# Sample tokens' low parts as extra columns of the first pass, in a split-float32 projection kernel

## The chip, the cores and the metric

The kernel runs on one core of a Trainium2 chip. The metric is the device time of one execution in microseconds. Times below are of the kernel before the change, from its timed runs and from one profiled execution.

## What is computed

One layer of a hybrid decoder on 256 prompt tokens and 8 single sample tokens (which come with a key/value window of 128 and with conv and SSM states), model width 2048, all in float32. Cut to what matters:

```python
def token_mixers(hn, pos, lw, state):
    proj = jnp.einsum('bld,de->ble', hn, lw['w_in'])
    q, k, v, z, xbc, dt_raw, gates = jnp.split(proj, SPLITS, axis=-1)
    q, k = rope(q, pos), rope(k, pos)              # 32 query heads, 8 key heads of 64
    attn = window_attn_...(q, k, v, sinks)         # window 128
    xbc_act, new_conv = causal_conv(xbc, conv_in, ...)
    y, h_last = ssd_chunked(...) or ssd_recurrent(...)
    y = gated_group_rms_norm(y + d_skip * xs, z, lw['ssm_norm'])
    attn_d = jnp.einsum('ble,ed->bld', attn, lw['w_attn_branch'])
    ssm_d = jnp.einsum('ble,ed->bld', y, lw['w_ssm_branch'])
    merged = sigmoid(g_attn) * attn_d + sigmoid(g_ssm) * ssm_d
    return jnp.einsum('bld,de->ble', merged, lw['w_out']), ...

def decoder_layer(x, pos, lw, state):
    mix, new_state = token_mixers(rms_norm(x, ...), pos, lw, state)
    h = x + rms_norm(mix, ...)
    g, u = split(rms_norm(h, ...) @ w_gate_up)
    return h + rms_norm((silu(g) * u) @ w_down, ...), new_state
```

## The kernel before

Activations lie with features on the partitions and tokens along the free axis: T = 264 columns, the NP = 256 prompt tokens first, then the NS = 8 sample tokens. A chunk is 128 features, so an activation of 2048 features is 16 tiles of 128x264.

All large products go through `gemm` (L143 to L187). A float32 product is made of three products of a shorter format: each weight piece is split into a rounded high part `hi` (a cast on ScalarE, L173, or L170 where heads are permuted) and the rest `lo` (a subtraction on VectorE, L174 or L171); each activation chunk likewise, when it is made, into a high tile (names in H: XH, HH, FH ...) and a low tile (XL, HL, FL ...), which `chunks` sets up and mostly `split` fills. For each output chunk m of 128 rows and each input chunk kc three matmuls accumulate in one PSUM tile: hi x high (L183), hi x low (L184) and lo x high (L185), 264 columns each. The low x low product is left out. A product (one call of `gemm`) has up to four output chunks, so it takes four PSUM tiles (name `g`); there are five such buffers. Weights come in pieces of 4 x 128 rows by 512 columns (`raw`, 3 buffers), and are split in halves of 128x1024 elements (4 buffers each for `hi` and `lo`).

In order of time: the pre-norm and the transposes of the input; the SSD branch's products (B, C, dt, x, z) with its conv and chunked scan, to 600 us; keys, values and queries from 600 us on, with the rotary embedding (`rope`), the prompt's attention and the sample tokens' recurrence beside them (both are generators of which `tick`, at each step of a product, lets some steps go ahead); the gates to 980 us; the SSM branch's projection (activations Y) to 1189 us; the attention branch's (A) to 1285 us; the output projection (M) to 1381 us, its norm; gate and up (H) from 1389 to 1915 us; the down projection (F) to 2177 us, the last norm and the output.

Readers of a finished `g` differ by stage: copies on ScalarE, the first conv step, and in the FFN a multiplication of gate and up on VectorE (L967 f). L309 and L477 are small copies of the 8 sample columns out of `g`.

The order of instructions on each engine is settled when the program is built, by the framework's scheduler, which simulates the engines and takes what it expects to be ready; an engine then runs its list in that order.

Of the kernel before, what the change touches and what calls it, by code (L numbers as in the profile page):

```python
# [5 lines left out]
F32R = mybir.dt.float32r  # L6
I32 = mybir.dt.int32
AF = mybir.ActivationFunctionType
ALU = mybir.AluOpType
# [23 lines left out]
def build(tc, I, O, wbufs=(3, 4, 4), gbufs=5, sbufs=((3,), (1, 2), (3,)), woff=0, aux="gpsimd", rr=1.4, pr=1.2, su=2, sr=1.0, hb=5, xbb=2, x0g=(0, 1, 2, 3), x0st="sync"):  # L33
# [81 lines left out]
    def chunks(pl, nm, n):  # L115
        r = [], []
        for c in range(n):
            for a, x in zip(r, "HL"):
                a.append(til(pl, [P, T], f"{nm}{x}{c}", 1, F32R))
        return r  # L120

# [21 lines left out]
    def gemm(W, segs, nk, X, perm_heads=False, perm_rows=False):  # L143
        XH, XL = X
        w = sum(n for _, n in segs)
        nch = w // P
        ps = [gps() for _ in range(nch)]
        for g0 in range(0, nk, 4):
            raw = til(wp, [P, 4, 512], "raw", wbufs[0])
            with tc.high_priority(offset=woff):  # L150
                o = 0
                for c0, n in segs:
                    src = W[g0 * P:(g0 + 4) * P, c0:c0 + n]
                    if perm_rows:
                        for j in range(2):
                            dma(raw[64 * j:64 * j + 64, :, o:o + n],
                                src[256 * j:256 * j + 256].rearrange("(i d) n -> d i n", d=64))
                    else:
                        last[0] = dma(raw[:, :, o:o + n], src.rearrange("(k p) n -> p k n", p=P))
                    o += n  # L160
                hl = []
                for b in range(2):
                    hi = til(wp, [P, 2, 512], "hi", wbufs[1], F32R)
                    lo = til(wp, [P, 2, 512], "lo", wbufs[2], F32R)
                    r = raw[:, 2 * b:2 * b + 2, :w]
                    if perm_heads:
                        for k in range(2):
                            rk = r[:, k].rearrange("p (j i d) -> p j i d", j=2, i=4)
                            hk, lk = (a[:, k].rearrange("p (i j d) -> p j i d", j=2, i=4) for a in (hi, lo))
                            S.copy(hk, rk)  # L170
                            V.tensor_tensor(lk, rk, fr(hk), ALU.subtract)  # L171
                    else:
                        S.copy(hi[:, :, :w], r)  # L173
                        V.tensor_tensor(lo[:, :, :w], r, fr(hi[:, :, :w]), ALU.subtract)  # L174
                    hl.append((hi, lo))
            for b in range(2):
                hi, lo = hl[b]
                for m in range(nch):
                    for k in range(2):
                        kc = g0 + 2 * b + k  # L180
                        wh, wl = (a[:, k, m * P:(m + 1) * P] for a in (hi, lo))
                        f, l = kc == 0, kc == nk - 1
                        PE.matmul(ps[m][:, :T], wh, XH[kc], start=f, stop=False)  # L183
                        PE.matmul(ps[m][:, :T], wh, XL[kc], start=False, stop=False)  # L184
                        PE.matmul(ps[m][:, :T], wl, XH[kc], start=False, stop=l)  # L185
            tick()
        return ps  # L187

# [1 line left out]
    win = I["w_in"]  # L190
# [11 lines left out]
    XHp = pool("xhat", side="right")  # L202
    XH, XL = chunks(XHp, "X", 16)
    SR = pool("srec")
# [47 lines left out]

# [1 line left out]
    ss = til(cp, [P, 3], "ss")  # L254
# [40 lines left out]
    A0.release()  # L295
    X = (XH, XL)

# [1 line left out]
    MS = til(cp, [P, 2, 8], "MS")  # L299
# [17 lines left out]
    def decays():  # L317
# [1 line left out]
        dtT = til(cp, [P, T], "dtT")  # L319
# [175 lines left out]

# [1 line left out]
    ps = sps()  # L497
# [13 lines left out]

# [1 line left out]
    cwb = lambda k: cw[:, k, :].unsqueeze(1).broadcast_to([P, NS, 48])  # L513
# [8 lines left out]

# [1 line left out]
    psum_phase(1)  # L524
# [65 lines left out]

# [1 line left out]
    def rope(pss, dsts):  # L592
# [47 lines left out]

# [1 line left out]
    QB = til(A4, [P, NS, 4, 8], "QB")  # L642
# [65 lines left out]

# [1 line left out]
    def sample_attention():  # L710
# [65 lines left out]

# [1 line left out]
    for dst, c0 in ((ts_d, C_GS), (ta_d, C_GA)):  # L778
# [9 lines left out]

# [1 line left out]
    psum_phase(2)  # L790
    YP = pool("yp", side="right")
    YH, YL = chunks(YP, "Y", 32)
    DP = pool("dproj", side="right")
# [12 lines left out]
    for u4 in range(4):  # L806
        for i, ps in enumerate(gemm(I["w_ssm_branch"], [(512 * u4, 512)], 32, (YH, YL))):
            m = 4 * u4 + i
            t = til(DP, [P, T], "ts", 3)
            ld(t, ts_d[m])  # L810
            V.scalar_tensor_tensor(t, t, 1.0, ps[:, :T], ALU.add, ALU.mult)
            st(m1_d[m], t)
        if u4 == 2:
            drain()
            SA.release()
            A4.release()
            AO = pool("attn_o")
            AH, AL = chunks(AO, "A", 16)
            for c in range(16):
                split(AF_[c], AH[c], AL[c])  # L820
    DP.release()
    YP.release()

# [1 line left out]
    MP = pool("merged", side="right")  # L825
    MH, ML = chunks(MP, "M", 16)
    DP = pool("dproj2")
    for u4 in range(4):
        for i, ps in enumerate(gemm(I["w_attn_branch"], [(512 * u4, 512)], 16, (AH, AL), perm_rows=True)):
            m = 4 * u4 + i  # L830
# [11 lines left out]

# [1 line left out]
    HP = pool("hp")  # L844
    HH, HL = chunks(HP, "H", 16)
    rb2 = til(HP, [P, T], "rb2")
# [28 lines left out]
    for u4 in range(4):  # L875
        for i, ps in enumerate(gemm(I["w_out"], [(512 * u4, 512)], 16, (MH, ML))):
            m = 4 * u4 + i
# [28 lines left out]

# [1 line left out]
    def gate(u4):  # L908
        sgs = []
        for ps in gemm(I["w_gate_up"], [(512 * u4, 512)], 16, (HH, HL)):  # L910
            sg = til(FT, [P, T], "sg", 8)
# [37 lines left out]
    FP = pool("fp", side="right")  # L949
    FH, FL = chunks(FP, "F", 44)  # L950

# [8 lines left out]
    for u4 in range(11):  # L960
        if u4 > 1:
            sgs.append(gate(u4))
            if u4 < 10:
                keep(u4 - 2)
        for i, ps in enumerate(gemm(I["w_gate_up"], [(DFF + 512 * u4, 512)], 16, (HH, HL))):
            f = til(FT, [P, T], "f", 3)
            V.tensor_tensor(f, ps[:, :T], sgs[u4][i], ALU.mult)  # L967
            split(f, FH[4 * u4 + i], FL[4 * u4 + i])
# [7 lines left out]
    for u4 in range(4):  # L976
        fw = til(GP, [P, 4, T], "fw", 1)
        for i, ps in enumerate(gemm(I["w_down"], [(512 * u4, 512)], 44, (FH, FL))):
            m = 4 * u4 + i
# [106 lines left out]
```

## Time and profile before

| what | value |
|---|---|
| timed runs | 2193.24, 2193.39, 2197.06 us |
| median | 2193.39 us |
| span of the profiled execution | 2195.1 us |
| TensorE busy | 2157.2 us, 98%, 17513 matmuls |
| VectorE busy | 1381.5 us, 63% |
| ScalarE busy | 1114.4 us, 51% |
| matmuls of `gemm` (L183, L184, L185) | 5328 each, 264 columns |

A busy time is the sum over an engine's instructions without their overlaps; matmuls overlap in the pipeline, so a matmul's own duration (0.28 us) is longer than the distance from one start to the next. The trace tells what released an engine that had been idle (an arrow in the rows), and a list in order of time gives the chain of work that ended last. Some matmul records are missing from a trace, so counts in a stretch can be a little low.

### The profile page before, as it was taken

What the parts mean: (1) busy time and instruction counts of PE and PEld (TensorE: products, weight loads), DVE (VectorE), ACT (ScalarE), POOL (GpSimd) and SP (SyncE); (2) the same over time, 40 slices, a digit from 0 to 9 for tenths busy, and PEclk for the clock granted to TensorE, in tenths of its full rate; (3) what the DMA queues carried; (4) which work ended last, traced back from release to release, by engine and by line L of the source; (5) the groups of instructions that cost most, each with busy time, mean ns of one, the idle gap of its engine ahead of it and who ended that gap; (6) DMA issues with size and microseconds to landing.
All of it is one profiled execution on the core that took longest, in us unless ns stands there. A gap on an engine that the chain in (4) does not pass through costs nothing.

```text
span 2195.1 us, 43269 instructions
## 1 busy us (share of the span) xinstructions
PE 2157.2 (98%) x17513; PEld 2114.8 (96%) x17513; DVE 1381.5 (63%) x2762; ACT 1114.4 (51%) x1987; POOL 294.6 (13%) x561
## 2 busy tenths in 40 slices
PE   8999999999999999999999999899999999999997
PEld 7999999999999999999999999899999999999997
DVE  5877777777689877857544554844554544544444
ACT  5555555555588866745533344554444444434442
POOL 4101111110132322343011120210000000000000
PEclk9999999999999999999999999999999999999998
DMA  5665565555687677777557985355555555555553
GB/s 192 232 200 187 190 194 180 190 188 188 198 303 235 220 259 237 245 267 239 169 204 186 218 269 175 131 201 199 194 194 192 186 199 185 180 186 173 174 175 135
DMA packets 208713, 442.65 MB, mean 202 GB/s; under 512 B 12448, under 2 KB 17968, under 8 KB 207720
## 3 DMA queue, kind: packets, MB, share of 16 engines
q1 hardware_dynamic: 183888, 363.07, 51.3%
q0 software_dynamic: 24624, 76.81, 10.7%
q8 instruction: 137, 2.24, 0.4%
q14 instruction: 64, 0.52, 0.1%
HBM read 402.87 MB, written 41.52 MB: 202 GB/s over the span
## 4 chain that ended last, share of the span: by engine, by line
PE 95%; DMA 2%; DVE 2%; issue 0%; ACT 0%; POOL 0%; SPq 0%; DVEq 0%; ACTq 0%
PE g L185 29%; PE g L183 29%; PE g L184 29%; DMA raw<-in_w_attn_branch 1%; PE s L651 1%; PE s L691 1%; PE s L269 1%; PE s L684 0%; PE s L464 0%; DVE HL L901 0%; DMA xt<-in_x_prompt 0%; PE s L756 0%; PE s L435 0%; PE s L422 0%; PE s L468 0%
## 5 line engine op out<-in xcount | busy, mean ns | idle before, releaser
L174 DVE TENSOR_TENSOR lo<-raw,hi 128x1024 fp32r<-128x1024 f32 (+1 forms) x640 | 776.2, 1216 | 605.9 <-ACT hi L173 605.1
L173 ACT CAST hi<-raw 128x1024 fp32r<-128x1024 f32 (+1 forms) x640 | 664.3, 1041 | 868.8 <-PE g L184 772.1
L183 PE MATMUL g<-XH,hi 128*128 128x264 f32 x2192 | 628.8, 289 | 1.8 <-ACT hi L173 1.8
L184 PE MATMUL g<-XL,hi 128*128 128x264 f32 x2192 | 629.8, 288 | 0.0
L185 PE MATMUL g<-XH,lo 128*128 128x264 f32 x2192 | 625.7, 288 | 0.1
L184 PEld LDWEIGHTS g<-XL,hi 128*128 128x128 f32 x2192 | 415.5, 190 | 5.2 <-issue 3.7
L183 PEld LDWEIGHTS g<-XH,hi 128*128 128x128 f32 x2192 | 412.7, 189 | 6.2 <-issue 2.5
L185 PEld LDWEIGHTS g<-XH,lo 128*128 128x128 f32 x2192 | 412.4, 189 | 4.9 <-issue 3.1
L184 PE MATMUL g<-HL,hi 128*128 128x264 f32 x1408 | 398.6, 285 | 1.9 <-DVE HL L901 1.9
L185 PE MATMUL g<-HH,lo 128*128 128x264 f32 x1408 | 397.8, 285 | 0.1
L183 PE MATMUL g<-HH,hi 128*128 128x264 f32 x1408 | 392.9, 286 | 1.8 <-ACT HH L894 1.8
L184 PEld LDWEIGHTS g<-HL,hi 128*128 128x128 f32 x1408 | 267.1, 190 | 2.8 <-DVE HL L901 2.7
L185 PEld LDWEIGHTS g<-HH,lo 128*128 128x128 f32 x1408 | 265.0, 189 | 0.4 <-DVE lo L174 0.3
L183 PEld LDWEIGHTS g<-HH,hi 128*128 128x128 f32 x1408 | 261.4, 188 | 1.9 <-ACT HH L894 1.8
L183 PE MATMUL g<-FH,hi 128*128 128x264 f32 x704 | 201.0, 286 | 0.0
L185 PE MATMUL g<-FH,lo 128*128 128x264 f32 x704 | 200.1, 285 | 0.0
L184 PE MATMUL g<-FL,hi 128*128 128x264 f32 x704 | 199.6, 284 | 0.0
L185 PE MATMUL g<-YH,lo 128*128 128x264 f32 x512 | 147.4, 289 | 0.0
L184 PE MATMUL g<-YL,hi 128*128 128x264 f32 x512 | 146.6, 287 | 0.7 <-DVE YL L90 0.7
L183 PE MATMUL g<-YH,hi 128*128 128x264 f32 x512 | 146.3, 289 | 0.0
L184 PEld LDWEIGHTS g<-FL,hi 128*128 128x128 f32 x704 | 133.1, 189 | 0.0
L185 PEld LDWEIGHTS g<-FH,lo 128*128 128x128 f32 x704 | 132.2, 188 | 0.1
(406 smaller groups left out, 3095.1 us busy)
## 6 DMA issues: line engine op xcount, KB each, us to landing
raw<-in_w_in SPq DMA_DIRECT2D x136, 1024.0 KB, 5.2
raw<-in_w_gate_up SPq DMA_DIRECT2D x88, 1024.0 KB, 5.0
raw<-in_w_down SPq DMA_DIRECT2D x44, 1024.0 KB, 5.1
raw<-in_w_ssm_branch SPq DMA_DIRECT2D x32, 1024.0 KB, 5.2
h<-in_state_ssm POOLq DMA_DIRECT2D x64, 256.0 KB, 4.7
out_ssm_sample<-h POOLq DMA_DIRECT2D x64, 256.0 KB, 5.4
raw<-in_w_attn_branch SPq DMA_DIRECT2D x32, 512.0 KB, 10.9
raw<-in_w_out SPq DMA_DIRECT2D x16, 1024.0 KB, 5.1
```

What stands on the lines that cost most here:

```text
L173: S.copy(hi[:, :, :w], r)
L174: V.tensor_tensor(lo[:, :, :w], r, fr(hi[:, :, :w]), ALU.subtract)
L183: PE.matmul(ps[m][:, :T], wh, XH[kc], start=f, stop=False)
L184: PE.matmul(ps[m][:, :T], wh, XL[kc], start=False, stop=False)
L185: PE.matmul(ps[m][:, :T], wl, XH[kc], start=False, stop=l)
L269: PE.transpose(ps[:, t * P:t * P + n], xts[t][:n, c * P:(c + 1) * P], ident[:n, :n])
L651: PE.matmul(pS[j][:, P:384], qt[jj[j], P:NP], kT[c][jj[j], 0:NP], start=True, stop=True)
L691: PE.matmul(po[jj[j], 0:NP], Vk[:, 0, vc[j]], pT[j][:, 0:NP], start=True, stop=False)
```

## The change

Each activation chunk becomes one tile of 528 columns: 264 low columns, then 264 high ones. Columns 256 to 527 of it are the 8 sample tokens' low parts, followed by all the high parts. The three matmuls of a (m, kc) are now:

- `both` (L183): hi x the 272 columns from 256 on, into PSUM columns 0 to 271;
- `low` (L186): hi x the prompt's 256 low columns, into PSUM columns 8 to 263;
- `high` (L189): lo x the 264 high columns, into PSUM columns 8 to 271.

The 8 columns at the front of the PSUM tile thus hold the sample tokens' hi x low sums, the 264 behind them everything else. For the last kc the order is high, low, both. When a chunk is complete, ScalarE copies the front columns into a small SBUF tile `sl` (L195) and VectorE adds them to the last 8 of the 264 (L196). `gemm` returns columns 8 to 271. Lines behind `gemm` move by 11 (L174 is L171 now, L967 is L978, L556 is L567, L672 is L683).

```diff
     def chunks(pl, nm, n):
-        r = [], []
-        for c in range(n):
-            for a, x in zip(r, "HL"):
-                a.append(til(pl, [P, T], f"{nm}{x}{c}", 1, F32R))
-        return r
+        hl = [til(pl, [P, 2 * T], f"{nm}{c}", 1, F32R) for c in range(n)]
+        return [a[:, T:] for a in hl], [a[:, :T] for a in hl], hl
...
     def gemm(W, segs, nk, X, perm_heads=False, perm_rows=False):
-        XH, XL = X
+        XX = X[2]
...
-                        PE.matmul(ps[m][:, :T], wh, XH[kc], start=f, stop=False)
-                        PE.matmul(ps[m][:, :T], wh, XL[kc], start=False, stop=False)
-                        PE.matmul(ps[m][:, :T], wl, XH[kc], start=False, stop=l)
+                        x = XX[kc]
+
+                        def both():
+                            PE.matmul(ps[m][:, 0:NS + T], wh, x[:, NP:], start=f, stop=l)
+
+                        def low():
+                            PE.matmul(ps[m][:, NS:T], wh, x[:, 0:NP], start=False, stop=False)
+
+                        def high():
+                            PE.matmul(ps[m][:, NS:NS + T], wl, x[:, T:], start=False, stop=False)
+
+                        for p in (high, low, both) if l else (both, low, high):
+                            p()
+                    if kc == nk - 1:
+                        sl = til(wp, [P, NS], "sl", 6)
+                        S.copy(sl, ps[m][:, 0:NS])
+                        V.tensor_tensor(ps[m][:, T:T + NS], ps[m][:, T:T + NS], sl, ALU.add)
             tick()
-        return ps
+        return [a[:, NS:NS + T] for a in ps]
```

The remaining edits hand the third list (`XX`, `YY`, `AA`, `MM`, `HX`, `FF`) to `gemm`.

The scheduler, with other instructions before it, also settles another order. On TensorE, at the boundary of two products in the FFN before the change (g_21814 to g_21817 are one product's four output chunks; right of the arrow stand the activation and the weight tile):

```order
L183 MATMUL g_21814<-HH_2431_16355,hi_21824 128x264
L184 MATMUL g_21814<-HL_2432_16356,hi_21824 128x264
L185 MATMUL g_21814<-HH_2431_16355,lo_21825 128x264
L183 MATMUL g_21815<-HH_2429_16353,hi_21824 128x264
L183 MATMUL g_21816<-HH_2425_16349,hi_21820 128x264
L184 MATMUL g_21816<-HL_2426_16350,hi_21820 128x264
L185 MATMUL g_21816<-HH_2425_16349,lo_21821 128x264
L183 MATMUL g_21816<-HH_2427_16351,hi_21820 128x264
L184 MATMUL g_21816<-HL_2428_16352,hi_21820 128x264
L185 MATMUL g_21816<-HH_2427_16351,lo_21821 128x264
L184 MATMUL g_21815<-HL_2430_16354,hi_21824 128x264
```

The first two output chunks are two weight halves ahead when the third one begins.

Such a boundary after the change, where g_20313 and g_20314 are the first two output chunks of a product:

```order
L183 MATMUL g_20313<-H_2518_16780,hi_20377 128x272
L186 MATMUL g_20313<-H_2518_16780,hi_20377 128x256
L189 MATMUL g_20313<-H_2518_16780,lo_20378 128x264
L183 MATMUL g_20313<-H_2519_16781,hi_20377 128x272
L186 MATMUL g_20313<-H_2519_16781,hi_20377 128x256
L189 MATMUL g_20313<-H_2519_16781,lo_20378 128x264
L183 MATMUL g_20314<-H_2514_16776,hi_20319 128x272
L186 MATMUL g_20314<-H_2514_16776,hi_20319 128x256
L189 MATMUL g_20314<-H_2514_16776,lo_20320 128x264
```

Here the first output chunk takes three weight halves (the last is hi_20377) before the second one begins: the lead of the first chunk has grown, and the second has none.

On VectorE at such a boundary, before:

```order
L174 TENSOR_TENSOR lo_21825<-raw_21818,hi_21824 128x1024
L967 TENSOR_TENSOR f_21798<-g_21562,sg_21547 128x264
L174 TENSOR_TENSOR lo_21879<-raw_21876,hi_21878 128x1024
L967 TENSOR_TENSOR f_21802<-g_21563,sg_21550 128x264
L90 TENSOR_TENSOR FL_2753_18261<-f_21798,FH_2752_18260 128x264
L967 TENSOR_TENSOR f_21806<-g_21564,sg_21553 128x264
L967 TENSOR_TENSOR f_21810<-g_21565,sg_21556 128x264
L174 TENSOR_TENSOR lo_21883<-raw_21876,hi_21882 128x1024
L90 TENSOR_TENSOR FL_2755_18263<-f_21802,FH_2754_18262 128x264
L90 TENSOR_TENSOR FL_2757_18265<-f_21806,FH_2756_18264 128x264
L90 TENSOR_TENSOR FL_2759_18267<-f_21810,FH_2758_18266 128x264
```

Readers of g (L967) and weight subtractions (L174) alternate.

And after (L196 is the new addition, L978 the multiplication that was L967):

```order
L171 TENSOR_TENSOR lo_20378<-raw_20375,hi_20377 128x1024
L196 TENSOR_TENSOR g_20049<-g_20049,sl_20267 128x8
L196 TENSOR_TENSOR g_20050<-g_20050,sl_20276 128x8
L196 TENSOR_TENSOR g_20051<-g_20051,sl_20285 128x8
L978 TENSOR_TENSOR f_20297<-g_20049,sg_20034 128x264
L978 TENSOR_TENSOR f_20301<-g_20050,sg_20037 128x264
L978 TENSOR_TENSOR f_20305<-g_20051,sg_20040 128x264
L196 TENSOR_TENSOR g_20052<-g_20052,sl_20294 128x8
L171 TENSOR_TENSOR lo_20382<-raw_20375,hi_20381 128x1024
L90 TENSOR_TENSOR F_2805_18699<-f_20297,F_2805_18699 128x264
L90 TENSOR_TENSOR F_2806_18700<-f_20301,F_2806_18700 128x264
L90 TENSOR_TENSOR F_2807_18701<-f_20305,F_2807_18701 128x264
```

The additions of three output chunks stand together now, ahead of the first chunk's reader L978, and the subtractions ahead of them and behind.

On VectorE during the queries' products, after the change (L571 and L567 are steps of the sample recurrence, L683 one of the prompt's softmax; the four g are one product's output chunks):

```order
L571 ISA xb_8600,ysb_8584<-h_1305_8598,cx_8571 128x128
L571 ISA ysb_8584 128x1
L196 TENSOR_TENSOR g_9005<-g_9005,sl_9414 128x8
L196 TENSOR_TENSOR g_9006<-g_9006,sl_9423 128x8
L567 SCALAR_TENSOR_TENSOR h_1317_8686<-h_1317_8686,dcol_808,xb_8688 128x512
L683 TENSOR_TENSOR den_9346<-den_9346,esk_9345 128x4
L196 TENSOR_TENSOR g_9007<-g_9007,sl_9432 128x8
```

The additions are strewn among the steps of the recurrence and the softmax, where nothing stood for these chunks before.

## Rows read from the trace of the kernel before

**Rows 1.** The page: engine, busy us, share, instructions; granted clock

```profile
PE 2157.2 (98%) x17513; PEld 2114.8 (96%) x17513; DVE 1381.5 (63%) x2762; ACT 1114.4 (51%) x1987; POOL 294.6 (13%) x561
...
PEclk9999999999999999999999999999999999999998
```

**Rows 2.** The page's chain that ended last: by engine, then by line

```profile
PE 95%; DMA 2%; DVE 2%; issue 0%; ACT 0%; POOL 0%; SPq 0%; DVEq 0%; ACTq 0%
PE g L185 29%; PE g L183 29%; PE g L184 29%; DMA raw<-in_w_attn_branch 1%; PE s L651 1%; PE s L691 1%; PE s L269 1%; PE s L684 0%; PE s L464 0%; DVE HL L901 0%; DMA xt<-in_x_prompt 0%; PE s L756 0%; PE s L435 0%; PE s L422 0%; PE s L468 0%
```

**Rows 3.** What TensorE waited for: us in total, times, longest

```profile
PE g L183 <- DVE ts L835: 2.7, 1, 2.7
```

**Rows 4.** Timeline in the FFN: start, duration, engine, instruction, count

```profile
1500.09 0.28 PE L184 MATMUL g<-HL,hi 128*128 128x264 f32 x1
1500.10 0.19 PEld L185 LDWEIGHTS g<-HH,lo 128*128 128x128 f32 x1
1500.21 0.28 PE L185 MATMUL g<-HH,lo 128*128 128x264 f32 x1
...
1500.46 0.28 PE L184 MATMUL g<-HL,hi 128*128 128x264 f32 x1
```

**Rows 5.** Stretches: us, busy of PE, PEld, DVE, ACT, POOL, clock, DMA

```profile
121.00:600.00 479.00, 479.00 (x4107) 471.78 (x4106) 357.21 (x627) 253.49 (x446) 56.50 (x119) 1.00 0.59 189
600.00:660.00 60.00, 60.00 (x492) 59.15 (x490) 50.17 (x176) 49.16 (x120) 21.25 (x41) 1.00 0.88 303
660.00:690.00 30.00, 30.00 (x235) 28.58 (x235) 28.71 (x103) 27.47 (x75) 7.74 (x14) 1.00 0.75 247
690.00:720.00 30.00, 30.00 (x227) 27.67 (x226) 26.49 (x104) 26.26 (x75) 6.73 (x19) 1.00 0.63 200
...
1420.00:1925.00 505.00, 505.00 (x4152) 504.61 (x4152) 259.04 (x317) 218.25 (x277) 6.51 (x12) 1.00 0.58 191
1925.00:2181.00 256.00, 255.82 (x2114) 254.95 (x2112) 107.64 (x106) 99.86 (x121) 0.00 (x0) 1.00 0.50 169
```

**Rows 6.** TensorE's timeline at the lower clock, and that stretch's busy times

```profile
1034.68 0.42 PE L185 MATMUL g<-YH,lo 128*128 128x264 f32 x1
1034.90 0.42 PE L183 MATMUL g<-YH,hi 128*128 128x264 f32 x1
...
1034.00:1039.00 5.00, 5.00 (x25) 5.00 (x24) 2.02 (x10) 1.63 (x9) 3.15 (x10) 0.50 0.55 179
```

**Rows 7.** TensorE's timeline: narrow matmuls at 138 us, weight loads at 1029 us

```profile
138.44 1.05 PE L435 MATMUL s<-Bk,X 128*128 128x128 f32 x8
...
1029.07 2.99 PEld L756 LDWEIGHTS s<-spt,vb 128*128 128x128 f32 x26
```

**Rows 8.** Timeline at the FFN's start, and group of the low halves

```profile
1406.27 0.39 PE L184 MATMUL g<-HL,hi 128*128 128x264 f32 x1 [0.86 <-DVE HL L901]
...
L901 DVE SCALAR_TENSOR_TENSOR HL<-xr,vecs,HH 128x264 fp32r<-128x264 f32 x16 | 10.8, 675 | 0.2 <-ACT HH L894 0.2
```

**Rows 9.** Groups by line, the smallest of their kind: count, busy, mean ns

```profile
L309 ACT COPY RS<-g 128x8 f32<-128x8 f32 x48 | 8.7, 181 | 0.0
...
L672 DVE TENSOR_TENSOR den<-den,esk 128x4 f32<-128x4 f32 x16 | 2.5, 157 | 3.7 <-ACT sm L671 3.0 <-ACT esk L668 0.4
```

**Rows 10.** The timeline at the kernel's end

```profile
2176.93 0.39 ACT L865 ACTIVATE sqe<-g 128x264 f32<-128x264 f32 x1 [0.34 <-PE g L185]
...
2180.53 0.16 DVE L108 TENSOR_TENSOR r3t<-r3y 128x3 f32<-128x3 f32 x1
2180.73 0.16 DVE L109 TENSOR_TENSOR r3t<-r3t,r3h 128x3 f32<-128x3 f32 x1
```

**Rows 11.** Timeline of VectorE, then ScalarE, at a chunk's end (FFN)

```profile
1492.84 1.22 DVE L174 TENSOR_TENSOR lo<-raw,hi 128x1024 fp32r<-128x1024 f32 x1
1493.97 0.42 DVE L967 TENSOR_TENSOR f<-g,sg 128x264 f32<-128x264 f32 x1
...
1494.62 1.05 ACT L173 CAST hi<-raw 128x1024 fp32r<-128x1024 f32 x1 [1.20 <-PE g L184]
```

More of the change, by code (lines that the diff above doesn't have):

```diff
@@ L202, in build @@
     XHp = pool("xhat", side="right")
-    XH, XL = chunks(XHp, "X", 16)
+    XH, XL, XX = chunks(XHp, "X", 16)
     SR = pool("srec")
@@ L295, in build @@
     A0.release()
-    X = (XH, XL)
+    X = (XH, XL, XX)
     MS = til(cp, [P, 2, 8], "MS")
@@ L791, in build @@
     YP = pool("yp", side="right")
-    YH, YL = chunks(YP, "Y", 32)
+    YH, YL, YY = chunks(YP, "Y", 32)
     DP = pool("dproj", side="right")
@@ L806, in build @@
     for u4 in range(4):
-        for i, ps in enumerate(gemm(I["w_ssm_branch"], [(512 * u4, 512)], 32, (YH, YL))):
+        for i, ps in enumerate(gemm(I["w_ssm_branch"], [(512 * u4, 512)], 32, (YH, YL, YY))):
             m = 4 * u4 + i
@@ L817, in build @@
             AO = pool("attn_o")
-            AH, AL = chunks(AO, "A", 16)
+            AH, AL, AA = chunks(AO, "A", 16)
             for c in range(16):
@@ L825, in build @@
     MP = pool("merged", side="right")
-    MH, ML = chunks(MP, "M", 16)
+    MH, ML, MM = chunks(MP, "M", 16)
     DP = pool("dproj2")
     for u4 in range(4):
-        for i, ps in enumerate(gemm(I["w_attn_branch"], [(512 * u4, 512)], 16, (AH, AL), perm_rows=True)):
+        for i, ps in enumerate(gemm(I["w_attn_branch"], [(512 * u4, 512)], 16, (AH, AL, AA), perm_rows=True)):
             m = 4 * u4 + i
@@ L844, in build @@
     HP = pool("hp")
-    HH, HL = chunks(HP, "H", 16)
+    HH, HL, HX = chunks(HP, "H", 16)
     rb2 = til(HP, [P, T], "rb2")
@@ L875, in build @@
     for u4 in range(4):
-        for i, ps in enumerate(gemm(I["w_out"], [(512 * u4, 512)], 16, (MH, ML))):
+        for i, ps in enumerate(gemm(I["w_out"], [(512 * u4, 512)], 16, (MH, ML, MM))):
             m = 4 * u4 + i
@@ L909, in gate @@
         sgs = []
-        for ps in gemm(I["w_gate_up"], [(512 * u4, 512)], 16, (HH, HL)):
+        for ps in gemm(I["w_gate_up"], [(512 * u4, 512)], 16, (HH, HL, HX)):
             sg = til(FT, [P, T], "sg", 8)
@@ L949, in build @@
     FP = pool("fp", side="right")
-    FH, FL = chunks(FP, "F", 44)
+    FH, FL, FF = chunks(FP, "F", 44)
     def keep(b):
@@ L964, in build @@
                 keep(u4 - 2)
-        for i, ps in enumerate(gemm(I["w_gate_up"], [(DFF + 512 * u4, 512)], 16, (HH, HL))):
+        for i, ps in enumerate(gemm(I["w_gate_up"], [(DFF + 512 * u4, 512)], 16, (HH, HL, HX))):
             f = til(FT, [P, T], "f", 3)
@@ L977, in build @@
         fw = til(GP, [P, 4, T], "fw", 1)
-        for i, ps in enumerate(gemm(I["w_down"], [(512 * u4, 512)], 44, (FH, FL))):
+        for i, ps in enumerate(gemm(I["w_down"], [(512 * u4, 512)], 44, (FH, FL, FF))):
             m = 4 * u4 + i
```

## The prediction, made before the changed kernel was run

> **What bounds the kernel now.** I read the page's first two sections first: TensorE is busy for 2157.2 us of a span of 2195.1 us, at a mean granted clock close to full, while VectorE is busy 63% and ScalarE 51% [rows 1]. The chain of work that ended last agrees: 95% of it is TensorE, and three lines, L183, L184 and L185, hold 87% in equal parts [rows 2]. These are the three passes of the split product, and only what changes their rate, or makes TensorE wait, can move the time by much. Waits hardly exist: the largest entry for a matrix product in the list of what TensorE waited for is 2.7 us, once [rows 3].
>
> So the rate has to be understood. In the timeline of a steady stretch [rows 4] a weight load starts as soon as the matmul before it has started, and the next matmul follows 0.12 us later; from 1500.09 to 1500.46 three passes take 0.37 us, and over the FFN window 4152 recorded matmuls fill 505 us [rows 5], 0.1216 us each. At a granted clock of 0.50 (1.2 GHz) the starts lie exactly 0.22 us apart [rows 6], which is 264 columns at one column a cycle; so at 2.4 GHz 264 columns need 0.110 us, and 0.0116 us of the pitch is something else. A pass of few columns is not much cheaper: 8 matmuls of 128 columns take 1.05 us with the last one's own duration, some 0.28 us as in rows 4, (1.05 - 0.28)/7 = 0.110 us each, and 26 weight loads for matmuls of 8 columns take 2.99 us, (2.99 - 0.19)/25 = 0.112 us each [rows 7]. A matmul with its own weight load thus has a floor of about 0.112 us.
>
> **The change part by part.** There are 5328 triples (sums of the counts 2192, 1408, 704, 512, 256 and 256 of L183), in 289 output chunks of 128 rows: 137 from w_in, 16 each from the two branches, the output and the down projection, 88 from gate and up.
>
> *The passes.* Nothing is removed. A triple was 264 + 264 + 264 columns and is 272 + 256 + 264, the same 792, with the same three weight loads. If the pitch is columns at the clock's rate plus a constant, which is what lies nearest to rows 4 and 6 together, the triple costs what it cost: 0. The bounds are the two ways of not being a straight line. If the 0.0116 us belongs to what lies beyond 256 columns, the low pass falls from 0.1216 to the floor of 0.112 us: 5328 x 0.0096 = 51 us gained. If a pass of 256 gains nothing and one of 272 pays for its eight columns, 8/2.4 ns = 3.3 ns each, 5328 x 3.3 ns = 18 us are lost. I take 0.
>
> The rows show a load and a matmul overlapping and a pitch 11.6 ns above the columns. The Trainium skill ("TensorE: Matmul & The Clock Gate", section "Wait — 56ns, not 53.3ns?") gives a warm matmul its columns at 2.4 GHz plus a fixed 2.5 ns or so, whatever the width; by it the pass of 264 would take 112.5 ns, where rows 4 and 5 have 121.6, so the measurement decides on the size. Since its rule is a straight line, the triple would cost the same by it as well, which speaks against the gain from the 256-column pass.
>
> *The first pass waits for the low half.* It now reads 8 low columns, so its first use of a chunk needs the low part too. In the steady state those are long there. Where a stage starts on activations that are just being made it costs: at the FFN's start the first pass needed the high halves alone, and the second waited for the low ones, up to 0.86 us a time [rows 8]. The low half takes VectorE one 0.68 us step after the cast, so I add 0.7 us there and as much at the first product of the kernel; for each the bounds are 0 (the passes end waiting for the same low halves anyway) and 1.0.
>
> *The two small instructions for each chunk.* ScalarE copies 128x8 out of PSUM, VectorE adds it back. The copy has a twin in the trace, 181 ns at L309; for the add the nearest is a 128x4 addition at 157 ns [rows 9]. Over the kernel that is 289 x 0.181 = 52 us on ScalarE and 289 x 0.157 = 45 us on VectorE. Spread evenly it is hidden by TensorE: in the FFN window VectorE works 259 of 505 us, in the down projection 108 of 256, in the SSD stretch 357 of 479 [rows 5].
>
> It isn't hidden where VectorE is full. Between 660 and 720 us, where the queries' products, the prompt's attention and the sample recurrence run together, VectorE is busy 28.71 + 26.49 of 60 us and ScalarE 27.47 + 26.26 [rows 5], and in the stretch ahead of it 50.17 of 60. The 24 chunks of keys, values and queries fall there: 24 x 0.157 = 3.8 us more on VectorE and 24 x 0.181 = 4.3 us on ScalarE, into some 5 us of free time that is cut into pieces. What is late next are the weights' low parts (`lo`), which VectorE makes behind these adds, and TensorE waits for them. In the new order on VectorE three such adds stand between the recurrence's steps. Bounds: 0, if the weight buffers carry it, and 24 us, if each add also waits behind one 0.68 us subtract of this stretch (24 x (0.16 + 0.18 + 0.68)). I take 6 us: all of VectorE's 3.8 and half of ScalarE's, nearest to the rows that show both engines at nine tenths.
>
> *The ends that nothing covers.* Where TensorE has no other work after a product, copy and add lie on the path: at the output projection's end before its norm, and at the kernel's end, where the last chunk goes on to its square and its scaling [rows 10]. Dependent small VectorE steps there start 0.20 us apart, so I take 0.2 for the add, 0.2 for the copy and 0.1 for one more hand-over: 0.5 us, twice.
>
> *The PSUM ring.* Five buffers serve four chunks, so a finished chunk must be read out before the next but one matrix product's chunk needs its buffer, 24 matmuls or 2.9 us later. Before, a reader of 0.42 us was enough, behind at most one subtract of 1.22 us [rows 11]. Now there are copy, add and reader: behind one cast and one subtract at the worst, 1.05 + 0.18 + 1.22 + 0.16 + 0.42 = 3.0 us. That just misses 2.9, but only if everything falls badly; the new orders also put adds of three chunks ahead of the first reader, 2 x 0.73 us later. The bounds are 0 and 0.3 us (that 0.1 and two hand-overs of 0.1) for each of the 73 products (289 chunks in fours), 22 us; I take 0 since VectorE has half of its time free in these stages.
>
> *Sum.* 0 + 1.4 + 6 + 1.0 + 0 = 8.4 us on the profiled 2195.1 us. The runs' median, 2193.39, lies 1.7 us below the profiled span, so the forecast is 2193.4 + 8.4 = 2202 us. Own range of this case: 2191 (all hidden, and a mean pitch 0.1 ns smaller through other addresses, 15984 x 0.1 ns = 1.6 us) to 2216.
>
> **Rivals.**
>
> *A kink at 256 columns.* The low pass drops to the floor. Full effect: 2202 - 51 = 2151 us; half of it, 2176. For it: the 0.0116 us above the column time is unexplained, and the 128-column matmuls sit at 0.110 us. Against it: at 1.2 GHz the pass costs its columns to the hundredth, with no rounding up, and a constant per matmul explains rows 4 as well. Chance 0.24. It is the case on the other side, faster, and it decides from the point at which the low pass is 1.6 ns or more shorter than the high pass is lengthened (8.4 us / 5328).
>
> *The wide pass pays, the narrow one doesn't.* If the load and its hand-over set the pitch, 256 columns bring nothing, and 272 columns cost 3.3 ns: 2202 + 18 = 2220 us. For it: the 8-column matmuls' floor of 0.112 us. Against: the pitch at 264 is above that floor, so columns seem to count already. Chance 0.07.
>
> *Late release of PSUM.* The copy and the add come behind casts and subtracts, and TensorE waits at the boundaries of products, 0.3 us x 73 = 22 us: 2224 us. For it: the sum of 3.0 against 2.9 us. Against: both engines are idle for half of the time in the stages with most of the products [rows 5]. Chance 0.07.
>
> **How the numbers follow.** The straight line with some un-hidden small work has 0.62 and gives the time, 2202 us. The range of 2150 to 2220 us takes in nearly all of that case, three quarters of the kink and the lower halves of the other two: 0.6 + 0.18 + 0.03 + 0.02, about 0.8. A difference of 0.2%, 4.4 us, is about what a measurement of this kernel can tell from no change. Faster by more than that (below 2189): the kink, 0.24, and a tail of the first case, 0.02. Within it: 0.13, the part of the first case in which nearly everything hides. Slower: the rest of that case, 0.47, with the two slow rivals, 0.14.
>
> **What would show it.** In the changed kernel's FFN window: starts 0.122 us apart on the mean and pass for pass 3 ns longer and shorter than the 264-column pass if the line is straight; a gap of 10 ns on the low pass if there is a kink; only the first pass longer if it is the wide pass. New groups of 128x8 copies and adds, 289 each, with 0.16 to 0.18 us. TensorE's waits: new entries on `lo` between 600 and 930 us of some 6 us in all; entries on the readers of `g` if PSUM comes late. The prediction is wrong if the mean pitch moves by more than 0.3 ns (15984 x 0.3 ns = 5 us) or if waits outside 600 to 930 us add up to more than 5 us.

## The result, and the profile after

The changed kernel is slower: 2208.21 us median of four runs (2205.27 to 2211.26) beside 2193.31 us, a ratio of 1.0057 with an interval of 1.0040 to 1.0074. Timed once more (e13 below) it gave 1.0059 (1.0044 to 1.0073). The profiled execution has a span of 2209.3 us, 14.2 us more than before. Its page (busy us of each engine, then the chain by line):

```profile
PE 2163.4 (98%) x17513; PEld 2121.1 (96%) x17513; DVE 1411.8 (64%) x3051; ACT 1140.0 (52%) x2276; POOL 278.4 (13%) x561
...
PE 54%; DVE 2%; DMA 2%; issue 1%; ACT 0%; POOL 0%; DVEq 0%; SPq 0%; ACTq 0%; POOLq 0%
PE g L183 18%; PE g L189 17%; PE g L186 17%; DMA raw<-in_w_attn_branch 1%; DMA ta_d<-tg 1%; DVE lo L171 0%; DMA out_ssm_sample<-h 0%; DVE H L912 0%; PE s L767 0%; DMA y<-y_d 0%; DVE xr L904 0%; DVE raw L1018 0%; PE s L949 0%; PE s L742 0%; ACT hi L170 0%
```

TensorE's busy time grew by 6 us (2157.2 before [rows 1]), VectorE's by 30 and ScalarE's by 26, and the shares hardly moved. The three passes still lead the chain, whose rows add up to much less of the span than before [rows 2], so I don't build on it. What TensorE waited for tells more (us in total, times, longest), from the same trace:

```profile
PE g L183 <- ACT tg L793: 7.2, 4, 4.8
...
PE g L183 <- DVE H L912: 4.8, 4, 2.4
...
PE g L183 <- ACT hi L170: 3.2, 2, 1.9
...
PE s L869 <- ACT sqe L876: 0.9, 1, 0.9
PE g L189 <- DVE lo L171: 0.8, 1, 0.8
...
PE g L189 <- DVE lo L168: 0.4, 1, 0.4
```

The first row has no counterpart in the list of before: ScalarE's reading of the finished gate chunks (L793), 7.2 us. ScalarE itself waited for stores of `tg`, the tile that this step writes, before the change as well, 11.1 us in seven waits between 740 and 985 us; after it these are 23.6 us in eight. What is new is that TensorE has to wait with it. H is the FFN's start, where [rows 8] had 0.86 us waits. The passes themselves did as forecast. In the FFN the three starts are 0.13, 0.12 and 0.12 us apart (start, duration, engine, line; x2 are two matmuls merged):

```profile
1599.80 0.29 PE L183 MATMUL g<-H,hi 128*128 128x272 f32 x1
1599.93 0.28 PE L186 MATMUL g<-H,hi 128*128 128x256 f32 x1
1600.05 0.41 PE L189 MATMUL g<-H,lo 128*128 128x264 f32 x2
1600.29 0.28 PE L186 MATMUL g<-H,hi 128*128 128x256 f32 x1
```

Over all recorded starts at full clock in the whole trace (over 5150 for each line, distances under 0.16 us) the mean distance from a pass to the next start is 125.5 ns for 272 columns, 118.6 ns for 256 and 122.2 ns for 264: 3.3 and 3.6 ns from the middle one, where eight columns at 2.4 GHz are 3.3 ns. But the sum of a triple is 366.3 ns, and was 365.6 ns.

Where the 14.2 us lie, as distances between the first matmuls of each stage in the two profiles (X: w_in, M: output projection, H: gate and up, F: down):

| stretch | before | after | difference |
|---|---|---|---|
| start to X | 25.6 | 26.5 | +0.9 |
| X to M | 1260.4 | 1271.6 | +11.2 |
| M to H | 102.7 | 104.0 | +1.3 |
| H to F | 526.8 | 527.1 | +0.3 |
| F to the last matmul on F | 261.1 | 261.5 | +0.4 |
| from there to the end | 18.5 | 18.6 | +0.1 |

The stages behind 1300 us, which hold nearly half of the products, grew by 0.7 us on their matrix products and by 1.3 at the output projection and its norm. Nearly everything lies between X and M, and there in two things. TensorE waits, and behind the longest wait the granted clock falls. That wait, in TensorE's timeline and in ScalarE's (an arrow names what ended the idle time before):

```profile
909.85 0.28 PE L189 MATMUL g<-X,lo 128*128 128x264 f32 x1
914.94 0.59 PE L183 MATMUL g<-X,hi 128*128 128x272 f32 x1 [4.81 <-ACT tg L793]
915.33 0.41 PE L186 MATMUL g<-X,hi 128*128 128x256 f32 x1
915.54 0.42 PE L189 MATMUL g<-X,lo 128*128 128x264 f32 x1
...
903.18 0.67 ACT L793 ACTIVATE tg<-g 128x264 f32<-128x264 f32 x2
903.73 1.28 ACT L566 ACTIVATE xb<-cx 128x128 f32<-128x128 f32 x4
914.50 0.39 ACT L793 ACTIVATE tg<-g 128x264 f32<-128x264 f32 x1 [9.49 <-DMA ta_d<-tg]
```

ScalarE stood still for 9.49 us because the buffer of `tg` that it wanted was still being stored; the readers of two finished chunks stood behind that, and TensorE had no PSUM tile to go on with. In the chain ahead of it (start, us, what) that store (`ta_d`) begins at 907.96 us, behind the recurrence's state transfers (`out_ssm_sample`) on GpSimd's queue, and takes 6.43 us to land:

```profile
898.57 7.75 DMA out_ssm_sample<-h
...
907.42 0.54 POOL out_ssm_sample L568
907.96 6.43 DMA ta_d<-tg
```

Busy times and the clock around it, and in the long stretches (us, busy of PE, PEld, DVE, ACT, POOL, then the clock):

```profile
914.00:921.00 7.00, 6.06 (x28) 5.12 (x29) 2.45 (x2) 3.66 (x7) 3.21 (x6) 0.51 0.55 173
...
780.00:960.00 180.00, 172.78 (x1280) 159.79 (x1279) 140.72 (x548) 116.73 (x314) 50.52 (x92) 0.97 0.74 245
960.00:1100.00 140.00, 138.73 (x1107) 137.77 (x1106) 85.69 (x189) 69.37 (x151) 38.30 (x89) 0.96 0.66 220
```

For 7 us behind the wait the clock is 0.51, 1.2 GHz, and the passes come 0.21 us apart and more. The same stretches of before:

```profile
780.00:960.00 180.00, 180.00 (x1373) 166.83 (x1372) 141.14 (x542) 116.19 (x299) 49.41 (x93) 1.00 0.77 256
960.00:1100.00 140.00, 137.02 (x1086) 136.32 (x1084) 85.47 (x172) 71.68 (x146) 42.96 (x88) 0.95 0.62 206
```

One minus the clock, times the length, is the time lost to it: 5.4 + 5.6 us after in these two stretches, 0 + 7.0 before. Summed over the traces from X to M, TensorE stands idle for 13.6 us after and 7.6 before, and the lower clock costs 13.7 us after and 6.8 before. The two together grew by 12.9 us, more than the 11.2 us, although the slower triple (the three passes of one m and kc; 2960 triples x 0.76 ns = 2.2 us) should come on top; the balance isn't explained.

Of the two, the waits belong to the kernel, and the clock's share changes from one execution to the next. In a second profile of the changed kernel (e13) TensorE is idle for 15.3 us, the clock costs 8.5 us, and X to M is still 9.4 us longer than before. The same wait, 4.2 us long there, has a shorter stretch at 1.2 GHz behind it, and behind the wait of 2.7 us that ends at 1242 us in the kernel before [rows 3] the clock didn't fall at all (first e13, then before):

```profile
914.00:921.00 7.00, 6.25 (x40) 5.71 (x41) 3.21 (x5) 4.56 (x7) 3.22 (x6) 0.76 0.57 188
...
1242.00:1249.00 7.00, 7.00 (x58) 7.00 (x59) 5.45 (x9) 3.23 (x6) 3.05 (x6) 1.00 1.06 207
```

### The profile page after: what moved, and what is told of

Its sections match the earlier page's. It is cut to its first block, busy times and chain, and to the rows that moved or that the text cites. A ratio compares the mean times of both kernels' runs of the same rounds, so it can differ in the third digit from the quotient of the medians.

```text
span 2209.3 us, 43812 instructions
## 1 busy us (share of the span) xinstructions
PE 2163.4 (98%) x17513; PEld 2121.1 (96%) x17513; DVE 1411.8 (64%) x3051; ACT 1140.0 (52%) x2276; POOL 278.4 (13%) x561
## 4 chain that ended last, share of the span: by engine, by line
PE 54%; DVE 2%; DMA 2%; issue 1%; ACT 0%; POOL 0%; DVEq 0%; SPq 0%; ACTq 0%; POOLq 0%
PE g L183 18%; PE g L189 17%; PE g L186 17%; DMA raw<-in_w_attn_branch 1%; DMA ta_d<-tg 1%; DVE lo L171 0%; DMA out_ssm_sample<-h 0%; DVE H L912 0%; PE s L767 0%; DMA y<-y_d 0%; DVE xr L904 0%; DVE raw L1018 0%; PE s L949 0%; PE s L742 0%; ACT hi L170 0%
## 5 line engine op out<-in xcount | busy, mean ns | idle before, releaser
L171 DVE TENSOR_TENSOR lo<-raw,hi 128x1024 fp32r<-128x1024 f32 (+1 forms) x640 | 776.1, 1216 | 606.6 <-ACT hi L170 603.2
L183 PE MATMUL g<-X,hi 128*128 128x272 f32 x2192 | 618.6, 293 | 10.1 <-ACT tg L793 7.2
L186 PE MATMUL g<-X,hi 128*128 128x256 f32 x2192 | 622.6, 285 | 0.0
L189 PE MATMUL g<-X,lo 128*128 128x264 f32 x2192 | 600.2, 290 | 0.5 <-DVE lo L168 0.4
L183 PEld LDWEIGHTS g<-X,hi 128*128 128x128 f32 x2192 | 407.2, 190 | 16.2 <-ACT tg L793 8.1
L186 PEld LDWEIGHTS g<-X,hi 128*128 128x128 f32 x2192 | 416.7, 190 | 5.3 <-issue 4.3
L189 PEld LDWEIGHTS g<-X,lo 128*128 128x128 f32 x2192 | 401.9, 190 | 5.1 <-issue 3.0
L183 PE MATMUL g<-H,hi 128*128 128x272 f32 x1408 | 394.5, 290 | 5.0 <-DVE H L912 4.8
L186 PE MATMUL g<-H,hi 128*128 128x256 f32 x1408 | 395.4, 281 | 0.0
L189 PE MATMUL g<-H,lo 128*128 128x264 f32 x1408 | 386.3, 285 | 0.0
L186 PEld LDWEIGHTS g<-H,hi 128*128 128x128 f32 x1408 | 266.4, 189 | 0.1
L183 PEld LDWEIGHTS g<-H,hi 128*128 128x128 f32 x1408 | 259.5, 188 | 6.0 <-DVE H L912 3.4
L189 PEld LDWEIGHTS g<-H,lo 128*128 128x128 f32 x1408 | 259.4, 189 | 0.0
L183 PE MATMUL g<-F,hi 128*128 128x272 f32 x704 | 200.8, 289 | 0.0
L189 PE MATMUL g<-F,lo 128*128 128x264 f32 x704 | 198.3, 285 | 0.0
L186 PE MATMUL g<-F,hi 128*128 128x256 f32 x704 | 198.3, 282 | 0.0
L183 PE MATMUL g<-Y,hi 128*128 128x272 f32 x512 | 147.6, 293 | 0.0
L186 PE MATMUL g<-Y,hi 128*128 128x256 f32 x512 | 146.1, 285 | 0.0
L189 PE MATMUL g<-Y,lo 128*128 128x264 f32 x512 | 145.0, 289 | 0.0
L186 PEld LDWEIGHTS g<-F,hi 128*128 128x128 f32 x704 | 132.8, 189 | 0.0
L189 PEld LDWEIGHTS g<-F,lo 128*128 128x128 f32 x704 | 131.9, 189 | 0.1
```

Of the source, the lines that this page charges most:

```text
L183: PE.matmul(ps[m][:, 0:NS + T], wh, x[:, NP:], start=f, stop=l)
L186: PE.matmul(ps[m][:, NS:T], wh, x[:, 0:NP], start=False, stop=False)
L189: PE.matmul(ps[m][:, NS:NS + T], wl, x[:, T:], start=False, stop=False)
```

## The experiments

The pair is the ScalarE copy and the VectorE addition at a chunk's end. Each kernel was timed side by side with the kernel before, in four groups; that one's own median was 2193.3, 2195.9, 2196.5 and 2197.9 us in them, so ratios are compared. "X to M", "M to H" and "triple" are of one profiled execution of each kernel, which need not be a typical one: e7's is its longest (2210.1 us, median 2202.6) and e3's nearly its shortest (2195.8 us, median 2199.7). So differences of a few microseconds in "X to M" don't rank kernels. The triple does repeat: kernels with the same tiles agree within 0.1 ns.

| kernel | median us | ratio (interval) | X to M | M to H | triple, ns |
|---|---|---|---|---|---|
| before | 2193.3 | 1 | 1260.4 | 102.7 | 365.6 |
| after | 2208.2 | 1.0057 (1.0040 to 1.0074) | 1271.6 | 104.0 | 366.3 |
| after, once more (e13) | 2209.7 | 1.0059 (1.0044 to 1.0073) | 1269.8 | 104.9 | 366.3 |
| e1 pair, old passes | 2217.2 | 1.0097 (1.0084 to 1.0110) | 1275.9 | 105.6 | 365.6 |
| e2 new passes, no pair | 2204.3 | 1.0034 (1.0019 to 1.0049) | 1265.6 | 102.8 | 366.2 |
| e3 shared tile alone | 2199.7 | 1.0020 (1.0009 to 1.0031) | 1256.9 | 103.0 | 366.3 |
| e9 shared tile, 8 columns on | 2205.2 (one run) | | 1264.3 | 102.9 | 366.7 |
| e4 after, tg x 3 | 2204.0 | 1.0041 (1.0027 to 1.0056) | 1262.4 | 104.0 | 366.3 |
| e6 before, tg x 3 | 2212.0 | 1.0067 (1.0052 to 1.0081) | 1273.5 | 102.7 | 365.6 |
| e12 before, other steps | 2203.2 | 1.0025 (1.0017 to 1.0034) | 1268.7 | 102.7 | 365.6 |
| e7 after, pair first | 2202.6 | 1.0025 (1.0013 to 1.0038) | 1270.2 | 104.0 | 366.3 |
| e10 after, tg by ACT's queue | 2211.0 | 1.0062 (1.0049 to 1.0075) | 1267.4 | 104.0 | 366.3 |
| e11 after, no pair in w_in | 2202.5 | 1.0030 (1.0013 to 1.0046) | 1265.2 | 104.0 | 366.2 |

**The parts of the change.** The small pair on the old kernel:

```diff
                         PE.matmul(ps[m][:, :T], wl, XH[kc], start=False, stop=l)
+                    if kc == nk - 1:
+                        sl = til(wp, [P, NS], "sl", 6)
+                        S.copy(sl, ps[m][:, 0:NS])
+                        V.scalar_tensor_tensor(ps[m][:, NP:T], sl, 0.0, ps[m][:, NP:T], ALU.mult, ALU.add)
```

> The kernel before with its three passes of 264 columns, and only the small pair added for each output chunk: a ScalarE copy of 128x8 out of PSUM and a VectorE 128x8 operation that adds it back times zero. Theory (the passes are worth nothing, the pair is the cost, mainly through the orders and the waits of the stretch from 600 to 1000 us): 2202 to 2208 us, 0.4 to 0.7% above before. Rival (the cost lies in the passes or in the shared tiles): 2193 to 2196 us.

It is the slowest of all, 1.0097, beyond the theory's upper end, with nothing but the pair added. TensorE waits 3.8 us for the sample attention's `sT` and 3.4 for its `kt`, and 5.5 us for gate chunks; M to H is 2.9 us longer. The other half, the new passes without the pair (the sample columns lack hi x low):

```diff
-                    if kc == nk - 1:
-                        sl = til(wp, [P, NS], "sl", 6)
-                        S.copy(sl, ps[m][:, 0:NS])
-                        V.tensor_tensor(ps[m][:, T:T + NS], ps[m][:, T:T + NS], sl, ALU.add)
```

> The changed kernel with its passes of 272, 256 and 264 columns in shared tiles, but without the copy and the addition at a chunk's end, so the sample tokens lack the product of high weights and low activations. Theory: 2194 to 2200 us (the mean pitch of a triple is 0.7 ns longer in the changed kernel's trace, 5328 x 0.7 ns = 4 us, and the low half is awaited at a stage's start). Rival (the passes or the tiles are the cost): 2204 to 2208 us.

2204.3 us looks like the rival's lower end, but the kernel before took 2195.9 us beside it; on 2193.3 us its ratio, 1.0034, gives 2200.8 us, between the two ranges, and decides for neither. The two halves of the change don't add up either: 0.97% and 0.34% alone, 0.57% together. The triple is 366.2 ns; M to H is 102.8, so the pair at the output projection's end is what M to H pays for. Between X and M it loses 5.2 us. The shared tile alone:

```diff
-        r = [], []
-        for c in range(n):
-            for a, x in zip(r, "HL"):
-                a.append(til(pl, [P, T], f"{nm}{x}{c}", 1, F32R))
-        return r
+        hl = [til(pl, [P, 2 * T], f"{nm}{c}", 1, F32R) for c in range(n)]
+        return [a[:, T:] for a in hl], [a[:, :T] for a in hl]
```

> The kernel before with low and high part of a chunk in one tile of 528 columns, passes of 264 columns and no pair. Theory: 2193 to 2195 us. Rival (the shared tile makes the readers of one half wait for the writer of the other, or its addresses cost): 2197 us or more.

1.0020 (runs from 2194.9 to 2204.2 us): here the rival was right. The triple takes 366.3 ns with three passes of 264 columns, what it takes with 272, 256 and 264; so the widths cost nothing, and the 0.7 ns come with the shared tile. 5328 x 0.73 ns = 3.9 us, and the medians lie 3.8 us apart (2.0 to 6.8 us by the interval). In its profile the way from M's first matmul to the last one on F grew by 2.0 us, from 890.6 to 892.6, where 2368 triples ask for 1.7. X to M is shorter there in spite of the slower triple: the waits are those of before (7.0 us idle from 7.6), but the clock cost only 1.7 us instead of 6.8. To see whether it is the sharing or the place, the high part was moved on by 8 columns (`2 * T + 8`, high from `T + 8`):

> The kernel before with shared tiles of 536 columns, the high part 8 columns further on than in the shared tile of 528, passes of 264 columns, no pair. Theory (the 0.7 ns that a triple gained with the shared tile of 528 columns comes from where the parts lie in memory): the mean pitch of the three lines is again another one than 121.2, 122.4 and 122.7 ns, their sum between 364 and 368 ns. Rival (it comes from sharing a tile): the sum stays at 366.3 ns.

The three distances are 121.7, 121.5 and 123.4 ns, their sum 366.7: it changes with the place, though by little. Both kernels share a tile, so how much of the first 0.7 ns is the sharing itself, and which property of an address the rest hangs on, stays open.

**The waits.** A third buffer for `tg` in the changed kernel (`til(SA, [P, T], "tg", 3)`):

> The changed kernel with three instead of two buffers for the gates' tile tg. Theory (7 of the 15 us are TensorE waiting for ScalarE's gate reader L793, which itself waits for the store of an earlier tg behind the recurrence's state transfers): 2199 to 2204 us. Rival (the reader is late for the copies and additions ahead of it, whatever the buffers): 2206 to 2211 us.

The time is 1.0041, at the upper end of the theory's range, with an interval that overlaps with that of the changed kernel, so the times alone don't show a gain. TensorE's waits on `tg` are gone. Of the two longest that are left behind the pre-norm, the first stood there already (4.8 us), the second is new:

```profile
PE g L183 <- DVE H L912: 4.5, 4, 2.4
...
PE s L742 <- POOL kt L739: 4.0, 3, 2.8
```

The `kt` row belongs to the sample tokens' attention in the Y stage. X itself became 12 us shorter (951.6 from 963.7 us) and Y 5 us longer. The control, a third buffer in the kernel before, which has no pair and no new pass:

> The kernel before with three buffers for tg. Theory (before, the gates' reader was never late enough to hold TensorE, so the third buffer gives nothing by itself, and what time does move comes from another order): 2191 to 2196 us. Rival (the buffers are short before the change as well): 2185 to 2190 us.

Both ranges were missed; what fits is the theory's last clause, another order. A buffer that TensorE had never waited for made the kernel before 0.67% slower, as much as the whole change did. The scheduler had put some hundreds of TensorE's instructions in another order, and the recurrence (`lx`) and the sample attention (`kt`, 2.3 us in one wait before) came into TensorE's way; `ts` is hardly longer than before [rows 3]:

```profile
PE s L731 <- POOL kt L728: 5.3, 3, 2.5
...
PE s L565 <- DVE lx L563: 3.7, 1, 3.7
PE g L183 <- DVE ts L835: 3.0, 2, 2.6
```

```profile
780.00:960.00 180.00, 176.32 (x1332) 163.35 (x1331) 140.79 (x539) 116.24 (x299) 49.71 (x92) 0.99 0.75 246
960.00:1100.00 140.00, 133.28 (x1041) 132.01 (x1040) 78.70 (x160) 65.27 (x130) 39.95 (x84) 0.94 0.61 199
```

The clock is 0.94 between 960 and 1100 us, from 0.95 in the same stretch before and 0.99 in 780 to 960, where it was 1.00. From X to M TensorE is idle for 15.6 us and the clock costs 13.7 us, much as in the changed kernel, with the triple of before. A second control, the same instructions as before with the recurrence let ahead by another number (`rr=1.3` for `rr=1.4`):

> The kernel before with the sample recurrence let ahead at 1.3 instead of 1.4 steps for each tick: the same instructions in another order, no pair, passes of 264. Theory (the order in the stretch from 600 to 1300 us is worth as much as the whole change): another time than before by 3 us or more, 2198 to 2212 us, or below 2190, with the difference between X's and M's first matmul. Rival (the order before is as good as its neighbours): 2193 to 2197 us.

1.0025, as the theory has it: all of it is between X and M, 8.3 us, with 7.3 us of waits on `kt` (2.3 before). The gates' stores through another queue:

```diff
-                st(dst[4 * u4 + i], t)
+                nc.scalar.dma_start(dst[4 * u4 + i], t)
```

> The changed kernel with the gates' tiles tg stored through ScalarE's DMA queue instead of GpSimd's, where they stand behind the recurrence's state transfers. Theory (the waits of 5.1 and 2.1 us at 914.9 and 946.9 us come from there, and the fall of the granted clock behind them costs another 5 us): neither wait is there, 2197 to 2203 us. Rival (the time lost between 600 and 1300 us moves to other waits): 2204 to 2210 us, with the sum of that stretch unchanged.

The rival was right on the waits. Those at 914.9 and 946.9 us (5.1 and 2.1 us from start to start in the quote, 4.8 and 1.8 us of idle time) are gone, one of 4.1 us on the same reader is at 961 us and two of 4.5 us in sum on `kt` later; 1.0062 is the changed kernel's ratio. X to M, 1267.4 us, is 2 to 4 us shorter than in the changed kernel's two profiles, too little to tell by one profile. The pair issued with priority (the two instructions under `tc.high_priority()`):

> The changed kernel with the copy and the addition of each chunk issued at the scheduler's high priority. Theory (the 11 us beyond the tiles' 4 are waits between 600 and 1300 us that hang on where the pair and its neighbours stand in the order): the waits differ in place and sum, 2200 to 2212 us, and the stages from 1300 us on stay as they are. Rival (the pair's own time on two full engines is the cost, wherever it stands): 2206 to 2210 us, with the waits at the same places.

1.0025, with the waits elsewhere (785, 949, 964 and 973 us). So the pair's 97 us of instructions need not cost 15 us: with them in this order the whole change costs, within the intervals, what the shared tile costs alone (1.0020). It still isn't faster than before. Without the pair in w_in:

```diff
-                    if kc == nk - 1:
+                    if kc == nk - 1 and W is not win:
```

> The changed kernel without the copy and addition for the 137 output chunks of w_in, whose sample columns so lack the product of high weights and low activations; the pair stays for the other 152 chunks. Theory A (the pair costs where VectorE and ScalarE are full, from 600 to 960 us): no new waits there, 2199 to 2204 us. Theory B (the stretch from 600 to 1300 us pays for whatever order comes out, with or without a pair in it): anything from 2197 to 2212 us, made of waits in that stretch and of clock falls behind them. Under both the norm and the FFN's start, whose pair stays, cost what they cost in the changed kernel, 1.2 us more than without.

No wait of TensorE between 600 and 960 us is left in its list, as theory A has it, and the time, 1.0030, fits both. But X to M is 1265.2 us and not 1260: X is 949.1 us, shorter than before, and Y 221.7, longer by 13.7. It doesn't decide between them. M to H is 104.0 again, as forecast. The changed kernel once more:

> The changed kernel once more, as it is, beside the others of this call: 2204 to 2210 us; the waits at 914.9 and 946.9 us stay in place if they belong to its order, and the falls of the clock vary by one or two stretches, 1.7 to 3.4 us.

Its ratio is 1.0059. Idle times of 4.2 and 1.8 us stand at 914.7 and 945.3 us, so they belong to this order, not to a chance of the run. The falls of the clock vary, as forecast, and by more: 8.5 us lost from X to M, from 13.7.

**The price of columns.** The second pass of the old kernel on 208 columns (the low parts of 56 columns are left out):

```diff
-                        PE.matmul(ps[m][:, :T], wh, XL[kc], start=False, stop=False)
+                        PE.matmul(ps[m][:, :208], wh, XL[kc][:, :208], start=False, stop=False)
```

> The kernel before with the second pass cut to 208 columns, so the low parts of the last 56 columns are left out. Theory (a pass costs its columns at 2.4 GHz plus a constant of some 11.6 ns as long as that lies above the floor): the pass falls to 208/2.4 + 11.6 = 98 ns, 5328 x 23.5 ns = 125 us less, some 2068 us. Rival (a matmul with its own weight load takes at least 0.110 to 0.112 us): the pass stops at the floor, 5328 x 10 ns = 53 us less, some 2140 us.

2150.4 us in one run, between the two, nearer to the rival. Its timeline in the FFN (PEld are weight loads):

```profile
1450.39 0.28 PE L183 MATMUL g<-HH,hi 128*128 128x264 f32 x1
1450.51 0.26 PE L184 MATMUL g<-HL,hi 128*128 128x208 f32 x1
1450.52 0.19 PEld L185 LDWEIGHTS g<-HH,lo 128*128 128x128 f32 x1
1450.61 0.30 PE L185 MATMUL g<-HH,lo 128*128 128x264 f32 x1
1450.62 0.19 PEld L183 LDWEIGHTS g<-HH,hi 128*128 128x128 f32 x1
1450.75 0.29 PE L183 MATMUL g<-HH,hi 128*128 128x264 f32 x1
```

The narrow pass (L184) does take its columns plus a constant, 96 ns on the mean to the next start, 9 above 208/2.4. But the pass behind it, 264 columns as ever, now takes 138 ns, and the triple 354.4 instead of 365.6: of 23 ns in columns only 11 are kept. The weight loads of these two passes (L185 and the next L183) start 109 ns apart on the mean, while the narrow pass leaves 96 ns between the matmuls; so the next pass comes late because its load does, as far as the starts show. 5328 x 11.2 ns = 60 us, of which some is lost between X and M, where TensorE is idle for 16.1 us and the clock costs 13.7.

## Why the prediction came out

The forecast was 2202 us, the measurement is 2208.2 us, inside the range, on the forecast side; the sum was 8.4 us and the span grew by 14.2.

- *The passes, 0.* Right on the widths: no kink at 256 and no penalty for 272. The trace shows 125.5, 118.6 and 122.2 ns, and e3 with equal widths has the same sum. The case that could have made the change faster is gone with that, as is the wide-pass rival. What the step missed is the shared tile. I had allowed other addresses 0.1 ns for each matmul; they cost 0.25, 4.0 us in all. That is the term that failed in size. The floor of 0.112 us, on which the kink rests, isn't one for a single pass: the 208 columns of e5 take 96 ns, and the pass behind them pays.
- *The first pass waits for the low half, 0.7 twice.* The wait is there, a lasting cost isn't. At the FFN's start the distance from the last matmul of the norm to the first pass grew from 2.11 to 2.74 us. X begins 0.9 us later, but 0.4 of it is already there at the transposes ahead, and e9, with the old passes, begins X later still (26.6 us). At X's twelfth pass the changed kernel is 0.3 us behind, at the sixtieth ahead; in the FFN the delay has evened out by then too (H to F +0.3). That is the prediction's lower bound, 0, with the reason that it gave.
- *The pair's own times* are 167 ns each, from 181 and 157 forecast. Hidden in the FFN and the down projection, as forecast: +0.7 us on both, less than the slower triple alone asks for (2112 x 0.76 ns = 1.6 us).

```profile
L195 ACT COPY sl<-g 128x8 f32<-128x8 f32 x289 | 46.2, 167 | 88.9 <-PE g L183 88.1
...
L196 DVE TENSOR_TENSOR g<-g,sl 128x8 f32<-128x8 f32 x289 | 40.6, 167 | 22.7 <-ACT sl L195 20.2
```

- *The full stretch, 6 us.* A size of that order came, 11.2 us, but by luck: the reason is another. Waits on `lo` were to come between 600 and 930 us; there are 0.4 us of them there. What came is ScalarE's gate reader behind stores of `tg`, and the clock behind that, for which the sum had no term. Since kernels without any pair pay as much in the same stretch for another order (e6 13.1 us, e12 8.3 us), the runs don't show how much of the 11.2 us the pair itself asks for. X to M lies between 1256.9 and 1273.5 us in the five kernels with passes of 264 and no pair, and between 1262.4 and 1275.9 us in those with the pair everywhere: they overlap nearly wholly.
- *The ends, 0.5 twice.* The output projection's end cost 0.4 us (the wait on the square, 0.91 from 0.52 us), the kernel's end 0.1, half of the term in all.
- *The PSUM ring, 0.* Right for the FFN. But the rival's picture, a finished chunk read too late, is what happened at the gates; only it was a store that held the reader, not casts and subtracts, and it happened at four places, not 73.
- *The signs of being wrong.* The mean pitch moved by 0.25 ns, under the 0.3. The waits outside 600 to 930 us stand on the edge: between X and M TensorE has new ones of 5.1 us there, over the 5, while 5.7 us of before are gone, and the norm's end and the FFN's start add 1.5; on balance they grew by 1 us.

So the sign and the order of size were forecast on steps of which the ends held at half their size, the starts left no lasting cost, 4 us were missing, and 6 us had the wrong cause. That the time fell so well inside the range is in part luck.

## What to carry over

Columns that were only moved between passes brought nothing here: 272, 256 and 264 take what three times 264 take, as long as each pass lies above the pace of the weight loads (0.110 to 0.112 us, as worked out from [rows 7]). What is left is the helper instructions, and what they cost hung on the order: the pair gave 1.0097 on the old kernel, 1.0057 with the whole change, and 1.0025 with the pair put first. In a kernel whose order is planned anew at each build, measure a control that changes nothing but the order before a difference of half a per cent is put down to an edit, and profile a kernel twice before a stretch of one profile is explained. A wait of a few microseconds on the bounding engine can be paid twice, as the wait and again at the lower clock behind it, but how long the clock stays down differed between two executions of the same kernel.

## What the hardware showed that was not expected

A pass that is narrowed below the pace of the loads gives back time at the next pass: 96 ns and then 138 ns where 122 and 121 stood. And the same three matmuls of 264 columns take 365.6 ns with the low and high halves in two tiles, 366.3 in one tile of 528 columns and 366.7 in one of 536, 4 to 6 us in this kernel. A full account of the second isn't to be had from these runs.
